# A fused low-rank update on one core: loads of four tiles, and the two small matrices on another queue

## The chip, the cores and the metric

The kernel runs on one core of one Trainium2 chip. The metric is the device time of one execution in microseconds (us). It is taken from plain runs; the profile comes from one further execution, which has a time of its own.

## The reference, cut to what matters

```python
def reference(x, A, B, scale):
    lora = np.matmul(np.matmul(x, A), B)
    return (x + scale * lora).astype(np.float32)
```

x is 16 x 512 x 768 in float32, that is 8192 rows of 768 numbers. A is 768 x 16, B is 16 x 768, scale is 0.5. All of x is read once and an output of the same size is written once, 25.2 MB each way.

## The kernel before, in words

**Tiles and parts.** The 8192 rows make 64 tiles of 128 rows. All 64 stay in one SBUF buffer, `xs`, from their load to their store; no space is used twice, except that three tiles of the last load hold A, a transposed A and B until these have been converted. The tiles are grouped in six parts (`PARTS`, L14: 2, 6, 8, 16, 16, 16 tiles). Inside a part, partition p holds consecutive rows of x (`rows`, L77), so a load of n tiles moves one contiguous run of n x 3 KB for each of the 128 partitions. `LOADS` (L15) says how many tiles each load brings: 2, 6 and then seven times 8. `STORES` (L16) says in which order the parts are written back: part 2, 1, 0, 3, 4, 5, one store for each.

**Chunks.** The arithmetic runs over 16 chunks of 4 tiles. For each chunk: three casts of `xs` to float16 (`xh`, one for each 256 columns, L108; GpSimd does nearly all of them); 24 transposing matmuls against an identity (`xt_ps`, L212); six copies of the result to SBUF by ScalarE (`xt`, L168); six matmuls with A (`yt_ps`, L223); one scaled copy by ScalarE (`yt`, L159); eight matmuls with B, two for each tile (`lo_ps`, L232); and four additions by VectorE, which add `lo_ps` into `xs` in place (L191). TensorE's order is written out by hand (L238 to L269), the middle of it a loop over chunks.

**The first chunk.** Its three casts go to three engines at once: GpSimd (columns 0 to 255), VectorE (256 to 511, L175), ScalarE (512 to 767, L155). `narrowed` (L97) makes an engine wait for every load that holds a tile of the chunk, the first time that this engine needs that load. Before, chunk 0 has its tiles in loads 0 and 1.

**A and B.** GpSimd first zeroes the place of A (`a_rows`, L112, the first count of the semaphore `zeroed`). Then A and B are loaded. VectorE transposes A (L178), casts it in four pieces (`a_mm`, L183) and casts B (`b_mm`, L188). The last of these raises `prep`. TensorE's first matmul with A waits for `prep`, and so does the last load, since it overwrites the three borrowed tiles.

**Queues.** All transfers are issued by SyncE, in this order: load 0, load 1, a wait for `zeroed`, A, B, loads 2 to 7, a wait for `prep`, load 8, and then the six stores, each after a wait until its part has been summed (`added`, raised by VectorE at L195). Transfers that one engine issued start on the 16 DMA engines in the order of issue. GpSimd's last act is to wait for all stores (L150).

ScalarE's program starts at L153 with a wait for the identity and a one-column copy that draws its table load to the front; its cast for chunk 0 comes next. VectorE's program starts with the cast for chunk 0 (L175) and goes on with A and B.

Of the kernel before, what the change touches and what calls it, by code (L numbers as in the profile page):

```python
# [10 lines left out]

PARTS = [2, 6, 8, 16, 16, 16]  # L14
LOADS = [2, 6, 8, 8, 8, 8, 8, 8, 8]  # L15
STORES = [2, 1, 0, 3, 4, 5]  # L16

CHUNK = 4
# [3 lines left out]
def kernel(  # L22
# [8 lines left out]
    nc = tc.nc  # L31
# [14 lines left out]
    NB = D // 32  # L46
    assert D % W == 0 and sum(LOADS) == NT == sum(PARTS) and sorted(STORES) == list(range(len(PARTS)))
    n_splits = [(n0, min(512, D - n0)) for n0 in range(0, D, 512)]
# [20 lines left out]

    room = NT - LOADS[-1]  # L70
    a_rows = xs[0:32, room, 0 : 32 * R].rearrange("b (a r) -> b a r", r=R)
    a_t = xs[0:32, room + 1, 0 : 32 * R].rearrange("a (r b) -> a r b", r=R)
    b_f32 = xs[0:R, room + 2, :]

    starts = [sum(PARTS[:i]) for i in range(len(PARTS))]

    def rows(t2, t0, n):  # L77
        i = max(i for i in range(len(PARTS)) if starts[i] <= t0)
        part = t2[ds(starts[i] * P, PARTS[i] * P), :].rearrange("(p s) d -> p s d", s=PARTS[i])
        return part[:, ds(t0 - starts[i], n), :]  # L80

    with tc.tile_critical():  # L82
# [3 lines left out]
        S = {k: nc.alloc_semaphore(name=f"s_{k}") for k in names}  # L86
        landed = [nc.alloc_semaphore(name=f"s_load{i}") for i in range(len(LOADS))]
        stored = nc.alloc_semaphore(name="s_stored")
        part_of = [i for i, n in enumerate(LOADS) for _ in range(n)]

        def load(i):
            t0, n = sum(LOADS[:i]), LOADS[i]
            nc.sync.dma_start(out=xs[:, t0 : t0 + n, :], in_=rows(x2, t0, n)).then_inc(landed[i], 16)  # L93
# [3 lines left out]
        def narrowed(engine, c, u):  # L97
            for i in sorted({part_of[c * CHUNK + s] for s in range(CHUNK)}):
                if (engine.engine, i) not in known:
                    known.add((engine.engine, i))  # L100
                    engine.wait_ge(landed[i], 16)  # L101
            src = xs[:, ds(c * CHUNK, CHUNK), ds(u * W, W)]
            if c >= 1:
                engine.wait_ge(S["turned"], ND * (c - 1) + 2 * u + 2)
            if engine is nc.scalar:
                i = engine.copy(out=xh[u], in_=src)  # L106
            else:
                i = engine.tensor_copy(out=xh[u], in_=src)  # L108
            i.then_inc(S[f"fed{u}"], 1)
# [6 lines left out]
            out=ident, in_=ident, compare_op=mybir.AluOpType.not_equal, fill=1.0,  # L116
# [4 lines left out]
        nc.gpsimd.memset(yt, 0.0).then_inc(S["zeroed"], 1)  # L121


        load(0)
        load(1)
        nc.sync.wait_ge(S["zeroed"], 1)
        nc.sync.dma_start(
            out=a_rows[0:NB, :, :], in_=A.rearrange("(b a) r -> b a r", a=32)
        ).then_inc(S["a"], 16)
        nc.sync.dma_start(out=b_f32, in_=B).then_inc(S["b"], 16)  # L130
        for i in range(2, len(LOADS) - 1):
            load(i)
        nc.sync.wait_ge(S["prep"], 1)
        load(len(LOADS) - 1)
# [1 line left out]
        for i in STORES:  # L136
            t0, n = starts[i], PARTS[i]
            if i + 1 > summed_parts:
# [3 lines left out]
                out=rows(out2, t0, n), in_=xs[:, t0 : t0 + n, :]  # L142
# [7 lines left out]
        nc.gpsimd.wait_ge(stored, 16 * len(STORES))  # L150


        nc.scalar.wait_ge(S["ident"], 1)  # L153
        nc.scalar.copy(out=first, in_=ident[:, 0:1])  # L154
        narrowed(nc.scalar, 0, 2)  # L155
# [15 lines left out]

        ends = {sum(PARTS[: i + 1]) for i in range(len(PARTS))}
        for k in (0, 1, 3):
            nc.vector.sem_inc(S[f"freed{k}"], 1)
        narrowed(nc.vector, 0, 1)  # L175

        nc.vector.wait_ge(S["a"], 16)
        nc.vector.transpose(out=a_t, in_=a_rows.rearrange("b a r -> b r a")).then_inc(S["a_t"], 1)  # L178
# [3 lines left out]
        for k in range(4):  # L182
            nc.vector.tensor_copy(  # L183
                out=a_mm[ds(32 * k, 32), 0 : ND * R].rearrange("p (c r) -> p c r", r=R),
                in_=a_tv[:, k, :, :],
            )
        nc.vector.wait_ge(S["b"], 16)
        nc.vector.tensor_copy(out=b_mm[0:R, :], in_=b_f32).then_inc(S["prep"], 1)  # L188
        for k in range(NT):
            nc.vector.wait_ge(S["lora"], k + 1)  # L190
            nc.vector.tensor_tensor(  # L191
                out=xs[:, k, :], in0=xs[:, k, :], in1=lo_ps[k % 2], op=add
            ).then_inc(S[f"freed{(k + 2) % CHUNK}"], 1)
            if k + 1 in ends:
                nc.vector.drain().then_inc(S["added"], 1)  # L195
# [109 lines left out]
```

## Time and profile before

| | before |
|---|---|
| time, median of 3 runs | 124.5 us (124.44 to 124.58) |
| time of the profiled execution | 124.9 us |
| its span, first to last instruction | 123.1 us |
| around the span | 1.8 us |
| TensorE busy | 69.8 us, from slice 5 to slice 28 of 40 |
| VectorE, ScalarE, GpSimd busy | 60.0, 60.3, 51.1 us |
| DMA packets, bytes | 2231, 50.46 MB |
| share of the span in which the SyncE queue's packets were in work, mean of the 16 DMA engines | 96.3% |

The page of the profile gives each engine's busy time, then the span cut into 40 slices of 3.08 us with a digit for the busy tenths of each, then the DMA queues, the chain of work that ended last, groups of instructions by line, and the issues of transfers with the time from issue to landing. The trace behind it can be asked for a stretch of time: which instructions ran, how busy the DMA engines were and what they moved. In such a stretch a packet counts where it begins, so a short stretch can show a DMA share of more than 1. An average over the whole span hides that the kernel has stages with different limits, so the stages are looked at one by one.

### The profile page before, as it was taken

The numbers are of one execution on the slowest core, as the hardware profiler recorded it, in microseconds if no ns is written. First come the engines' busy times: TensorE is split into PE (matmuls) and PEld (weight loads), VectorE is DVE, ScalarE is ACT, GpSimd is POOL, SyncE is SP. The second block draws the span as 40 slices with busy tenths as digits, with TensorE's granted clock in tenths as the row PEclk, the third lists the DMA queues.
The fourth block names the chain that finished last, engine by engine and source line by source line (L and its number), as shares of the span: only waits on it lengthen the run. The fifth ranks groups of instructions, "written<-read, shape, count | busy, mean of one in ns | idle before, by whom it ended". The sixth has DMA issues, their size and how long they took to land.

```text
span 123.1 us, 1586 instructions
## 1 busy us (share of the span) xinstructions
PE 69.8 (57%) x608; PEld 42.9 (35%) x608; DVE 60.0 (49%) x71; ACT 60.3 (49%) x115; POOL 51.1 (42%) x56
## 2 busy tenths in 40 slices
PE   0000699999999999999999999973000000000000
PEld 0000556656666565666656665630000000000000
DVE  0002706879779877977897798779000000000000
ACT  4002569878987987798789779850000000000000
POOL 6102677678667767676786677100000000000000
PEclk9999999999999999999999999999755555555555
DMA  3999999999999999999999999999989979989970
GB/s 92 439 419 383 463 407 415 463 399 455 423 407 479 402 423 455 399 423 450 399 463 407 413 434 509 411 431 479 447 351 495 447 335 495 463 367 447 495 303 0
DMA packets 2231, 50.46 MB, mean 410 GB/s; under 512 B 268, under 2 KB 268, under 8 KB 564
## 3 DMA queue, kind: packets, MB, share of 16 engines
q1 hardware_dynamic: 2228, 50.43, 96.3%
q14 instruction: 3, 0.02, 0.0%
HBM read 25.26 MB, written 25.17 MB: 410 GB/s over the span
## 4 chain that ended last, share of the span: by engine, by line
PE 54%; DMA 8%; DVE 4%; ACT 1%; issue 1%; DVEq 1%; SPq 0%
PE lo_ps L232 20%; PE yt_ps L223 17%; PE xt_ps L212 17%; DMA xs<-in_x_dram 8%; DVE xs L191 2%; ACT xt L168 1%; DVE xs L178 1%; DVE a_mm L183 1%; DVEq L195 1%; ACT yt L159 0%; DVE b_mm L188 0%; SPq L93 0%; DVE xh L108 0%; SPq L300 0%; DVEq L101 0%
## 5 line engine op out<-in xcount | busy, mean ns | idle before, releaser
L191 DVE TENSOR_TENSOR xs<-xs,lo_ps 128x768 f32<-128x768 f32 x64 | 56.9, 950 | 14.9 <-PE lo_ps L232 14.7
L108 POOL CAST xh<-xs 128x1024 f16<-128x1024 f32 x46 | 48.6, 1057 | 25.3 <-PE xt_ps L212 16.3
L168 ACT CAST xt<-xt_ps 128x512 f16<-128x512 f32 x96 | 49.8, 578 | 4.1 <-PE xt_ps L212 1.7
L212 PE MATMUL xt_ps<-ident,xh 128*128 128x128 f16 x384 | 32.8, 223 | 13.2 <-POOL xh L108 13.2
L212 PEld LDWEIGHTS xt_ps<-ident,xh 128*128 128x128 f16 x384 | 27.6, 100 | 21.3 <-issue 13.7
L223 PE MATMUL yt_ps<-xt,a_mm 128*128 128x512 f16 x96 | 32.0, 384 | 0.2
L232 PE MATMUL lo_ps<-b_mm,yt 128*128 128x512 f16 (+1 forms) x128 | 29.1, 330 | 2.0 <-DVE xs L191 1.1
L223 PEld LDWEIGHTS yt_ps<-xt,a_mm 128*128 128x128 f16 x96 | 9.4, 98 | 11.3 <-ACT xt L168 5.4
L159 ACT ACTIVATE yt<-yt_ps 16x512 f16<-16x512 f32 x16 | 9.4, 587 | 7.8 <-PE yt_ps L223 7.8
L232 PEld LDWEIGHTS lo_ps<-b_mm,yt 128*128 128x128 f16 x128 | 8.6, 97 | 9.4 <-ACT yt L159 2.7
L108 DVE CAST xh<-xs 128x1024 f16<-128x1024 f32 x1 | 0.7, 694 | 11.5 <-DMA xs<-in_x_dram 11.5
L106 ACT CAST xh<-xs 128x1024 f16<-128x1024 f32 x1 | 1.0, 1045 | 9.1 <-DMA xs<-in_x_dram 9.1
L154 ACT ACT_TABLE_LOAD x1 | 1.3, 1283 | 0.9 <-SPq L82 0.9
L178 DVE STREAM_TRANSPOSE xs<-xs 32x512 f32<-32x512 f32 x1 | 1.0, 1040 | 0.0
L183 DVE CAST a_mm<-xs 32x96 f16<-32x96 f32 x4 | 0.9, 232 | 0.1
L120 POOL MEMSET b_mm<- 128x768 f16 x1 | 0.7, 738 | 0.0
L112 POOL MEMSET xs<- 32x512 f32 x1 | 0.5, 514 | 0.5 <-SPq L82 0.5
L188 DVE CAST b_mm<-xs 16x768 f16<-16x768 f32 x1 | 0.5, 548 | 0.0
L121 POOL MEMSET yt<- 128x512 f16 x1 | 0.5, 524 | 0.0
L115 POOL TENSOR_SCALAR_AFFINE_SELECT ident<-ident 128x128 f16<-128x128 f16 x1 | 0.3, 292 | 0.2 <-POOL ident L113 0.2
L119 POOL MEMSET a_mm<- 128x208 f16 x1 | 0.3, 272 | 0.0
L154 ACT COPY first<-ident 128x1 f16<-128x1 f16 x1 | 0.2, 194 | 0.0
(5 smaller groups left out, 0.6 us busy)
## 6 DMA issues: line engine op xcount, KB each, us to landing
xs<-in_x_dram SPq DMA_DIRECT2D x7, 3072.0 KB, 36.3
out_dram<-xs SPq DMA_DIRECT2D x3, 6144.0 KB, 38.0
out_dram<-xs SPq DMA_DIRECT2D x1, 3072.0 KB, 35.6
xs<-in_x_dram SPq DMA_DIRECT2D x1, 2304.0 KB, 10.0
out_dram<-xs SPq DMA_DIRECT2D x1, 2304.0 KB, 40.6
xs<-in_x_dram SPq DMA_DIRECT2D x1, 768.0 KB, 4.5
out_dram<-xs SPq DMA_DIRECT2D x1, 768.0 KB, 42.1
xs<-in_A_dram SPq DMA_DIRECT2D x1, 48.0 KB
```

The lines of the kernel that those rows point to most:

```text
L106: i = engine.copy(out=xh[u], in_=src)
L108: i = engine.tensor_copy(out=xh[u], in_=src)
L154: nc.scalar.copy(out=first, in_=ident[:, 0:1])
L159: nc.scalar.activation(out=yt[0:R, :], in_=yt_ps[0:R, :], func=mybir.ActivationFunctionType.Copy, scale=sc).then_inc(S["y"], 1)
L168: nc.scalar.copy(out=xt[j], in_=xt_ps[j % NX]).then_inc(S[f"got{j}"], 1)
L178: nc.vector.transpose(out=a_t, in_=a_rows.rearrange("b a r -> b r a")).then_inc(S["a_t"], 1)
L183: nc.vector.tensor_copy(out=a_mm[ds(32 * k, 32), 0 : ND * R].rearrange("p (c r) -> p c r", r=R), in_=a_tv[:, k, :, :],)
L191: nc.vector.tensor_tensor(out=xs[:, k, :], in0=xs[:, k, :], in1=lo_ps[k % 2], op=add).then_inc(S[f"freed{(k + 2) % CHUNK}"], 1)
L195: nc.vector.drain().then_inc(S["added"], 1)
L212: i = nc.tensor.matmul(xt_ps[j % NX][:, ds(s * P, P)], xh[u][:, s, ds(h * P, P)], ident, start=True, stop=True,)
L223: i = nc.tensor.matmul(yt_ps, a_mm[:, ds(j * R, P)], xt[j], start=(j == 0), stop=(j == ND - 1))
L232: i = nc.tensor.matmul(lo_ps[s % 2][:, ds(n0, w)], yt[:, ds(s * P, P)], b_mm[:, ds(n0, w)], start=True, stop=True,)
```

## The change

Five edits, given here as the diff with its context cut. The issue of A and B moves from SyncE's program to the head of ScalarE's, B first, since only A has to wait for the zeroed place. The first 40 tiles are loaded four at a time by ten loads and the remaining 24 by three loads of eight, so there are 13 loads in place of 9. The first three parts have 4, 4 and 8 tiles in place of 2, 6 and 8, so load 0 holds exactly chunk 0. VectorE's cast for chunk 0 moves behind its work on A and B. The number of stores and their order stay; the two small ones are of 4 and 4 tiles in place of 6 and 2. The last load still has eight tiles and waits for `prep`.

```diff
-PARTS = [2, 6, 8, 16, 16, 16]
-LOADS = [2, 6, 8, 8, 8, 8, 8, 8, 8]
+PARTS = [4, 4, 8, 16, 16, 16]
+LOADS = 10 * [4] + 3 * [8]
 STORES = [2, 1, 0, 3, 4, 5]
...
-        load(0)
-        load(1)
-        nc.sync.wait_ge(S["zeroed"], 1)
-        nc.sync.dma_start(
-            out=a_rows[0:NB, :, :], in_=A.rearrange("(b a) r -> b a r", a=32)
-        ).then_inc(S["a"], 16)
-        nc.sync.dma_start(out=b_f32, in_=B).then_inc(S["b"], 16)
-        for i in range(2, len(LOADS) - 1):
+        for i in range(len(LOADS) - 1):
             load(i)
         nc.sync.wait_ge(S["prep"], 1)
         load(len(LOADS) - 1)
...
+        nc.scalar.dma_start(out=b_f32, in_=B).then_inc(S["b"], 16)
+        nc.scalar.wait_ge(S["zeroed"], 1)
+        nc.scalar.dma_start(
+            out=a_rows[0:NB, :, :], in_=A.rearrange("(b a) r -> b a r", a=32)
+        ).then_inc(S["a"], 16)
         nc.scalar.wait_ge(S["ident"], 1)
         nc.scalar.copy(out=first, in_=ident[:, 0:1])
         narrowed(nc.scalar, 0, 2)
...
-        narrowed(nc.vector, 0, 1)
...
         nc.vector.tensor_copy(out=b_mm[0:R, :], in_=b_f32).then_inc(S["prep"], 1)
+        narrowed(nc.vector, 0, 1)
         for k in range(NT):
```

## The prediction, made before the changed kernel ran

> **What bounds the kernel now.** I read the slices of the span first, then the issues of transfers, then single stretches. The page's slices:
>
> ```profile
> PE   0000699999999999999999999973000000000000
> ...
> DMA  3999999999999999999999999999989979989970
> GB/s 92 439 419 383 463 407 415 463 399 455 423 407 479 402 423 455 399 423 450 399 463 407 413 434 509 411 431 479 447 351 495 447 335 495 463 367 447 495 303 0
> ```
>
> TensorE starts in slice 5 and is done in slice 28. The DMA engines work from slice 2 to slice 39 with hardly a gap, so the transfers set the time and the arithmetic lies beside them. To see where the transfers lose time I add to each issue its time to landing. The page's list groups them:
>
> ```profile
> xs<-in_x_dram SPq DMA_DIRECT2D x7, 3072.0 KB, 36.3
> out_dram<-xs SPq DMA_DIRECT2D x3, 6144.0 KB, 38.0
> out_dram<-xs SPq DMA_DIRECT2D x1, 3072.0 KB, 35.6
> xs<-in_x_dram SPq DMA_DIRECT2D x1, 2304.0 KB, 10.0
> out_dram<-xs SPq DMA_DIRECT2D x1, 2304.0 KB, 40.6
> xs<-in_x_dram SPq DMA_DIRECT2D x1, 768.0 KB, 4.5
> out_dram<-xs SPq DMA_DIRECT2D x1, 768.0 KB, 42.1
> ```
>
> Asked in narrow stretches, the trace gives each one alone. Issue plus time to landing, in us: load 0 0.94+4.5 = 5.4; load 1 1.38+10.0 = 11.4; B 2.34+9.4 = 11.7; loads 2 to 7 at 18.8, 26.1, 33.4, 40.7, 48.3, 55.6; load 8 14.73+49.2 = 63.9; stores of parts 2, 1, 0 at 71.2, 76.6, 78.6; of parts 3, 4, 5 at 93.1, 107.5 and 86.52+35.5 = 122.0. I call this the ladder. A large store is a step of 14.5 us for 16 tiles, so two tiles (768 KB) cost 1.81 us, and all 128 tile transfers 116.0 us. The other 6.0 us before 122.0 are: 0.94 before the first issue; 3.2 at the start (11.4 - 0.94 - 4 x 1.81); 0.3 for A and B; 1.05 in load 8's step (8.3 for 7.25); 0.35 in load 6's (7.6); 0.2 in part 0's store (2.0 for 1.81); rounding. Then come 1.1 us to the span's end and 1.8 around it: 124.9 us for the profiled execution. The median of the plain runs is 0.4 lower, 124.5, and I carry that difference over.
>
> Two places in the ladder matter. The first is the start, seen in stretches (columns: length, five engines, clock, DMA share, GB/s):
>
> ```profile
> 0.00:2.00 2.00, 0.00 (x0) 0.00 (x0) 0.00 (x0) 1.09 (x1) 1.03 (x7) 1.00 0.06 9
> 2.00:4.00 2.00, 0.00 (x0) 0.00 (x0) 0.00 (x0) 0.38 (x2) 1.48 (x4) 1.00 0.92 313
> 10.00:12.00 2.00, 0.00 (x0) 0.00 (x0) 0.51 (x1) 0.53 (x1) 0.48 (x1) 1.00 1.20 424
> 91.50:106.00 14.50, 0.00 (x0) 0.00 (x0) 0.00 (x0) 0.00 (x0) 0.00 (x0) 0.50 1.00 434
> ```
>
> The last row is the norm: share 1.00 for 434 GB/s. From 10 to 12 us, where load 2's first packets follow the small ones of A and B, share 1.20 bought 424; 424/434 would be 0.98, so packets took 0.22 x 2 = 0.44 us longer than they should. The second place is load 8. Asked for 55.6 to 64 us, the queues answer:
>
> ```profile
> q1 hardware_dynamic: 159, 3.51, 99.6%
> q14 instruction: 1, 0.01, 0.2%
> ```
>
> One of the three instruction packets on the page came in this stretch; the second came in load 6's stretch, the third at 72 to 77 us. Both late loads have one. A landing waits for the slowest of 16 engines, so one delayed engine shows in full, and later steps do not win it back.
>
> **The change, part by part.**
>
> *A and B off the middle.* Their step, 0.3 us, goes. They must still ride somewhere: until 2 us the engines are dark (share 0.06), and from 2 to 4 us a share of 0.08, 0.16 us, is idle. All in the dark would save 0.3, interleaved with load 0 nothing. B is issued at about 0.9 us, beside load 0; A waits for `zeroed` (GpSimd's first memset on `xs` ends at 1.46) and B's issue (0.34), so its 0.43 us issue ends near 1.9 and its packets come after load 0's first. I take -0.2. The Trainium skill, "DMA: Bandwidth & Descriptors", section "Issuing engines are not separate DMA queues", speaks against this edit: transfers from several engines interleave on the same 16, and a second issuer saves only issue time. By that rule this term is 0 and the sum 0.2 higher; no run here has two issuers yet.
>
> *The slow packets behind them.* With no small packets ahead of a large load in mid-queue, the 0.44 us should go; or they follow A and B into the start (0), or come on top of its slow packets (+0.4). I take -0.4, since packets from 2 to 4 us are slow already (share 0.92 for 313 GB/s).
>
> *Four more transfers, in smaller packets.* Loads 9 to 13; stores stay 6 (two of 1536 KB for 2304 and 768; 5.4+2.0 against 7.25, so 0 to -0.1). Price of one more: a 768 KB step exceeded its size by 0.2, a 3072 KB step by 0.05. 1536 KB lies between, and the eight packets of each DMA engine are what both share; nearer the larger row, 0.075. Four make +0.3; ends +0.2 and +0.8.
>
> *First transfers of four tiles for 2 and 6.* Of the start's 3.2 us, load 0 holds 2.7 (4.5 - 1.81) and load 1 0.5. I take 0; the 0.5 could go or double.
>
> *The chunk-0 chain.* Load 0 lands near 5.4 + 1.81 = 7.2 us; before, all three casts waited until 11.4. VectorE now does A and B first: 1.04 + 0.97 + 0.55 = 2.6 us, then its 0.69 us cast. If A and B land by 4.5 that is hidden; if they land with load 0, the cast ends at 10.5. TensorE starts at 9 to 10.5 instead of 13.2, so all sums come 2.5 to 4 us earlier, worth 0: part 5's store is issued at 86.5 while its forerunner lands at 107.5 (cover 21 us), part 2's at 35.6 while load 8 lands at 63.9 (28 us).
>
> *Queues.* SyncE: twelve loads at a median 0.45 us are issued by about 6.4 us, then it waits for `prep` as now (the waits of its queue give `SPq L93 <- DVE b_mm L188` 8.9 us); the last load has over 40 us of queued loads ahead of it, so cost 0. ScalarE: its wait for `zeroed` and two issues push the table load (1.28 us, now at 0.91) to about 1.9, ending near 3.2; behind it are the identity copy, the cast for load 0 (7.2) and every evacuation: 4 us of cover, cost 0. VectorE: behind its wait for A stand the cast and all additions, behind the cast TensorE; priced above.
>
> *The last-load delay.* Its 1.05 us I leave as it is (0). Instruction packets will come at other times, for the arithmetic runs ahead, and may meet other DMA engines: -1.0 to +1.0.
>
> **Sum:** -0.2 - 0.4 + 0.3 = -0.3. Profiled execution 124.9 - 0.3 = 124.6, median **124.2 us**.
>
> **Rivals.**
>
> 1. *The late engine is spared* (0.17). If no instruction packet strikes an engine that is late already, load 8's step falls to 7.3: another -0.7 to -1.0, about 123.4. For it: steps without such a packet are 7.3. Against: three packets came in the span and the program isn't shorter.
>
> 2. *Two queues at the start, slower* (0.25). Place: the DMA engines at 2 to 6 us, where small packets of the ScalarE queue alternate with load 0's. Price: the 0.4 us of slow packets stays, the 0.3 step isn't saved, the transfers cost +0.3 to +0.8: 124.8 to 125.3. It decides once B's packets get to the engines no sooner than load 0's, so that none rides in the dark. For it: both issues start at 0.91 to 0.94.
>
> 3. *A later delay* (0.08): an instruction packet strikes the last engine once more, +1.0 on the forecast: 125.2. Against: only two of the ladder's steps show it.
>
> 4. *A fixed time for every transfer* (0.02). By the widest row, 0.2 each, it would be the +0.8 above. The Trainium skill, same page, "Anatomy of one DMA", fits 2.0 us plus bytes at 436 GB/s per transfer on the GpSimd path; four would be an estimated 8 us, if nothing overlaps. The trace speaks against that: 3072 KB steps are 7.3 us, and the fit would make them about 9.2.
>
> 5. *Nothing moves* (0.10): what is saved ahead is lost again to the slowest engine, 124.3 to 124.7.
>
> **How the numbers follow.** The forecast has the remaining 0.38, own range 123.9 to 124.6. A measurement of this kernel can tell about 0.2%, 0.25 us, from no change. Below 124.25 lie rival 1 (0.17) and 0.25 of the forecast: faster 0.42. Within: 0.13 of the forecast, 0.10 of rival 5, 0.04 of rival 2's lower end: same 0.27. Slower: 0.21 of rival 2, rivals 3 and 4: 0.31. The range from 123.3 (rival 1) to 125.2 (rivals 2 and 3) leaves out about 2 in 10: larger moves of the delays, the wide ends of the start, and rival 4.
>
> **What the changed profile would show.** In the ladder: load 0 near 7.2 us, the first eight tiles (loads 0 and 1) near 11.4, 16 tiles near 18.3 instead of 18.8; steps of 1536 KB at 3.7; large stores still 14.5 apart. In the stretches: no surplus of DMA share around 10 to 12 us. TensorE's first matmul at 9 to 10.5. Wrong if the 16 tiles land later than 18.8 (rival 2), if steps of 1536 KB are over 3.8 (packets), or if the last load's step isn't 8.3 (instruction packets). What would overturn all of it is a gap in the DMA row before the last store, for then transfers no longer set the time.

## The result, and the profile after

The changed kernel is slower: 124.97 us in the median of 8 runs (124.47 to 125.11), against 124.47 us for 8 runs of the kernel before beside it. The ratio is 1.0032 with a 95% interval of 1.0019 to 1.0046. A second set of 5 runs, taken later with other kernels, gave 124.84 us and 1.0037 (1.0024 to 1.0051). The forecast was 124.2, a gain of 0.3; it became a loss of 0.4 to 0.5.

The slices of the changed kernel's page, as before: the arithmetic starts a slice earlier, and the DMA engines still work from slice 2 to slice 39.

```profile
PE   0007999999999999999999999750000000000000
...
DMA  3999999999999999999999999999999899899890
GB/s 74 400 403 437 413 429 433 421 429 421 425 429 419 457 457 409 441 427 417 441 427 425 401 429 481 469 449 433 401 481 449 369 481 449 385 449 465 385 449 0
```

The list of transfers on the same page (KB each, median us to landing):

```profile
out_dram<-xs SPq DMA_DIRECT2D x3, 6144.0 KB, 40.3
xs<-in_x_dram SPq DMA_DIRECT2D x10, 1536.0 KB, 21.0
xs<-in_x_dram SPq DMA_DIRECT2D x3, 3072.0 KB, 45.6
...
xs<-in_B_dram ACTq DMA_DIRECT2D x1, 48.0 KB, 4.0
```

B lands 4.0 us after its issue instead of 9.4. The profiled execution was one of the eight runs and the lowest of them, 124.47 us with a span of 122.7. The kernel before had been profiled in an execution of 124.9 us, above all its plain runs. Two single profiles would therefore have told the wrong story, so both kernels were profiled again. The ladder (issue plus time to landing, us) of the two further profiles of the kernel before and of both of the changed kernel:

| landed | before, 2nd and 3rd profile | changed, 1st and 2nd |
|---|---|---|
| 8 tiles | 11.37, 11.54 | 11.53, 11.61 |
| 16 tiles | 18.81, 18.96 | 18.91, 18.98 |
| 40 tiles | 40.72, 40.87 | 41.35, 41.36 |
| 64 tiles | 63.25, 63.39 | 63.66, 63.82 |
| last store | 121.47, 121.54 | 121.64, 121.96 |
| time of the execution | 124.29, 124.36 | 124.47, 124.78 |

At 16 tiles, where a gain of 0.5 had been forecast, the kernels are level. Between 16 and 40 tiles, where the changed kernel loads fours and the other eights, it falls behind by 0.5. After that the gap shrinks, to 0.42 at 64 tiles and 0.30 at the last store (means of two), and these four executions differ by 0.30 in time. They lie below the medians of their sets, those of the changed kernel further on average.

### The profile page after: what moved, and what is told of

It reads as the page before. It is cut to its first block, busy times and chain, and to the rows that moved or that the text cites. A ratio compares the mean times of both kernels' runs of the same rounds, so it can differ in the third digit from the quotient of the medians.

```text
span 122.7 us, 1592 instructions
## 1 busy us (share of the span) xinstructions
PE 70.7 (58%) x608; PEld 43.4 (35%) x608; DVE 59.9 (49%) x71; ACT 60.5 (49%) x115; POOL 50.4 (41%) x56
## 4 chain that ended last, share of the span: by engine, by line
PE 56%; DMA 5%; DVE 5%; DVEq 1%; issue 1%; ACT 0%; POOL 0%; POOLq 0%; SPq 0%
PE lo_ps L230 20%; PE xt_ps L210 18%; PE yt_ps L221 18%; DMA xs<-in_A_dram 5%; DVE xs L189 2%; DVE xs L175 1%; DVE a_mm L180 1%; DVEq L193 1%; DVE xh L108 1%; ACT yt L157 0%; DVE b_mm L185 0%; POOL xs L112 0%; POOLq L298 0%; POOL ident L113 0%; SPq L82 0%
## 5 line engine op out<-in xcount | busy, mean ns | idle before, releaser
L108 POOL CAST xh<-xs 128x1024 f16<-128x1024 f32 x46 | 47.9, 1042 | 23.4 <-PE xt_ps L210 19.0
L210 PE MATMUL xt_ps<-ident,xh 128*128 128x128 f16 x384 | 33.5, 225 | 10.0 <-POOL xh L108 9.1
L221 PE MATMUL yt_ps<-xt,a_mm 128*128 128x512 f16 x96 | 32.6, 395 | 0.0
```

The source lines that it names most:

```text
L210: i = nc.tensor.matmul(xt_ps[j % NX][:, ds(s * P, P)], xh[u][:, s, ds(h * P, P)], ident, start=True, stop=True,)
L221: i = nc.tensor.matmul(yt_ps, a_mm[:, ds(j * R, P)], xt[j], start=(j == 0), stop=(j == ND - 1))
```

## The experiments

Times are medians; "before" is the kernel before, run beside each (124.39 to 124.48 us).

### Is it the queue or the loads?

Three kernels part the change. The first only moves A and B:

```diff
@@ the kernel before
-        nc.sync.wait_ge(S["zeroed"], 1)
-        nc.sync.dma_start(out=a_rows[0:NB, :, :], ...)
-        nc.sync.dma_start(out=b_f32, in_=B).then_inc(S["b"], 16)
...
+        nc.scalar.dma_start(out=b_f32, in_=B).then_inc(S["b"], 16)
+        nc.scalar.wait_ge(S["zeroed"], 1)
+        nc.scalar.dma_start(out=a_rows[0:NB, :, :], ...)
         nc.scalar.wait_ge(S["ident"], 1)
```

> The kernel before with one edit: A and B are issued at the head of ScalarE's program instead of between SyncE's loads 1 and 2. Theory (the small transfers bring their slow packets with them wherever they go, and smaller loads cost the rest): 16 tiles land at 18.6 to 19.0 us as before (18.81), the median stays within 0.2 us of before. Rival (two issuing queues at the start are what makes the changed kernel slower): 16 tiles land at 19.2 or later and the median is 0.3 to 0.5 us above before.

Measured: 124.89 us, 1.0038 (1.0025 to 1.0051). 16 tiles land at 18.90. Each theory got half: the landing is the one's, the time the rival's. It was profiled a second time; see Repeats.

The second only changes the loads and the parts:

```diff
@@ the kernel before
-PARTS = [2, 6, 8, 16, 16, 16]
-LOADS = [2, 6, 8, 8, 8, 8, 8, 8, 8]
+PARTS = [4, 4, 8, 16, 16, 16]
+LOADS = 10 * [4] + 3 * [8]
```

> The kernel before with the new PARTS and LOADS alone; A and B stay on SyncE's queue behind the first two loads (again eight tiles). Theory (smaller loads cost): each 1536 KB load steps by 3.69 us instead of 3.65, in sum +0.3 for the loads, and the median is 0.25 to 0.5 us above before, the whole of the change's loss. Rival (two queues): within 0.15 us of before.

Measured: 124.90 us, 1.0041 (1.0028 to 1.0054); 16 tiles at 19.12, steps of 3.69, 40 tiles at 41.26. The loads alone cost what the whole change costs, as the theory said. The two halves do not add up, though: each costs 0.4 to 0.5 us, and so do both together.

The third keeps everything of the change but the many small loads:

```diff
@@ the changed kernel
-LOADS = 10 * [4] + 3 * [8]
+LOADS = [4, 4, 8, 8, 8, 8, 8, 8, 8]
```

> The changed kernel with loads of 4, 4 and then seven times 8 tiles, so that only the first two loads are small; A and B on ScalarE's queue, parts as in the changed kernel. Theory (smaller loads cost): steps of 3072 KB at 7.3 us, 16 tiles near 18.8, the median within 0.2 us of before. Rival (two queues): the median stays 0.3 to 0.5 us above before.

Measured: 124.53 us, 1.0014 (1.0005 to 1.0022), steps of 7.30, 16 tiles at 18.89. With these loads, two issuing queues are not what costs. Its twin has the same loads and A and B on SyncE's queue:

```diff
@@ the kernel before
-PARTS = [2, 6, 8, 16, 16, 16]
-LOADS = [2, 6, 8, 8, 8, 8, 8, 8, 8]
+PARTS = [4, 4, 8, 16, 16, 16]
+LOADS = [4, 4, 8, 8, 8, 8, 8, 8, 8]
```

> The kernel before with parts of 4, 4, 8, 16, 16, 16 and loads of 4, 4 and seven times 8 tiles; A and B stay on SyncE's queue behind the first two loads. Beside the kernel with the same loads and A and B on ScalarE's queue (0.14% above before) it prices the move of A and B alone. Theory (the move of A and B gains nothing): 124.4 to 124.7, within 0.2 us of that one. Rival (the move gains the predicted 0.6): 124.9 to 125.2.

Measured: 124.58 us, 1.0008 (0.9999 to 1.0017), 16 tiles at 19.07. Beside the third kernel this prices the move of A and B with loads of four in front: the 16 tiles land 0.18 us earlier with the move, and the time does not tell the two apart. The Trainium skill ("DMA: Bandwidth & Descriptors", "Issuing engines are not separate DMA queues") says that a second issuer saves issue time only. These two runs agree with it; the first kernel of this section, 0.4 to 0.5 us slower by the same move, does not follow from it (Repeats has what cost it).

### What small loads cost

```diff
@@ the changed kernel
-LOADS = 10 * [4] + 3 * [8]
+LOADS = 28 * [2] + [8]
```

> The changed kernel with 28 loads of two tiles and one of eight in place of ten of four and three of eight. Theory (a fixed cost for each transfer and packet): a 768 KB step of 1.865 to 1.885 us, in sum about 1 us more than the changed kernel, median 125.7 to 126.1. Rival (the loss of the changed kernel is in its late steps and not in the number of loads): median within 0.3 us of the changed kernel, 124.7 to 125.2.

Measured: 125.77 us, 1.0102 (1.0087 to 1.0118), in the page's list

```profile
xs<-in_x_dram SPq DMA_DIRECT2D x28, 768.0 KB, 21.1
```

and in the ladder steps of 1.88 almost throughout. So the same eight tiles cost 7.30 us as one load, 2 x 3.69 = 7.38 as two and 4 x 1.88 = 7.52 as four: 0.07 to 0.08 us for each further transfer, which is eight more packets for each of the 16 engines. Sixteen more transfers than in the changed kernel took 0.93 us, 0.06 each. The fit of the Trainium skill (same page, "Anatomy of one DMA", 2.0 us and the bytes for each transfer, stated for the GpSimd path) would have made that an estimated 32 us; for transfers that stand in a queue the trace does not bear it out.

Does the price also run the other way?

```diff
@@ the changed kernel
-LOADS = 10 * [4] + 3 * [8]
+LOADS = [4, 4, 8, 16, 16, 8, 8]
```

> The changed kernel with fewer, larger loads: 4, 4, 8, 16, 16, 8, 8 tiles. Theory (cost by transfer and packet): 6144 KB steps of 14.5 us, 16 tiles near 18.9, median 124.2 to 124.5, level with before or a little below. Rival (two issuing queues cost whatever the loads are): 124.8 or more.

Measured: 124.97 us, 1.0040 (1.0026 to 1.0054): missed. The first load of 16 tiles took the expected 14.54, the second, with an instruction packet in it, 14.97, and all 64 tiles had landed at 62.83, earlier than in either kernel. But the stores' steps were 7.45, 3.87, 3.90 and 15.16, together 1.2 us over the changed kernel's second profile (7.29, 3.63, 3.63, 14.60). Chunk 4 now waits for a load of 16 tiles, the arithmetic ends later (the last store is issued at 93.2 instead of 83.8), and I read from this that late steps which go with the arithmetic fall into the stores; no run here separates it. So late steps had to be understood.

### What makes single steps late

Each of the profiles so far has three packets of the instruction queue in its span, and the steps with the first two of them are late. The next kernel lengthens SyncE's program where SyncE is idle. The 1024 waits leave 512 more instructions in the trace, 545 on SyncE for 33:

```diff
@@ the changed kernel
         load(len(LOADS) - 1)
+        for _ in range(1024):
+            nc.sync.wait_ge(S["prep"], 1)
```

> The changed kernel with 512 more instructions on SyncE between the last load and the stores, waits that are long satisfied. They move no data and SyncE is idle there; they only make its instruction stream longer, so that four more instruction packets of 8 KB come by the DMA engines. Theory (an instruction packet makes the engine that carries it late, and the slowest engine sets the end): instruction packets 3 to about 7, new late steps of 0.2 to 0.7 us between 14 and 45 us, and the median up by 0.5 to 2 us, the more of them fall on one engine. Rival (instruction packets are harmless and the late steps have another cause): the median stays within 0.2 us of the changed kernel.

Measured: 127.27 us, 1.0235 (1.0220 to 1.0249), 2.4 us over the changed kernel. Its page's queues:

```profile
q1 hardware_dynamic: 2736, 50.33, 94.3%
q10 hardware_dynamic: 68, 0.10, 0.6%
q14 instruction: 7, 0.06, 0.1%
```

There are 7 instruction packets for 3 and no other byte more. 0.6 us for each is far more than the 0.3 us that 8 KB takes: in the trace the engine's next data packet, too, takes about 0.4 us longer. All four struck the same engine, as the ends show: one engine finished 2.46 us after the last but one, and the others no later than in the changed kernel's second profile (121.28 us against 121.45), where the two last engines finish within 0.05. The theory's mechanism held; the 2.4 us are above its range of 0.5 to 2.

Then I tried to take the third packet away, by moving nine casts from GpSimd, whose program fetches it, to VectorE:

```diff
@@ the kernel before, GpSimd's loop and VectorE's
-                if c >= 1 or u == 0:
+                if (c >= 1 or u == 0) and c < NC - 3:
                     narrowed(nc.gpsimd, c, u)
...
                 nc.vector.drain().then_inc(S["added"], 1)
+            if (k + 1) % CHUNK == 0 and NC - 3 <= (k + 1) // CHUNK + 1 < NC:
+                for u in range(NU):
+                    narrowed(nc.vector, (k + 1) // CHUNK + 1, u)
```

> The kernel before with the casts of the last three chunks moved from GpSimd to VectorE, ahead of the additions of the chunk before each; GpSimd's program is ten instructions shorter. Theory (an instruction packet delays the engine that carries it, and the third one, at 62 to 74 us, is fetched for GpSimd's program, since it came earlier wherever GpSimd had more waits): two instruction packets in the span instead of three, and the median 0.1 to 0.5 us below before. Rival (the third belongs to another program, or its engine is not the last to finish): three packets, or two and no change within 0.1 us.

Measured: 124.85 us, 1.0037 (1.0025 to 1.0048). The page counts two instruction packets in the span; the third, which had come at 73.9 us, now comes at 123.3, after the span's end, so it was GpSimd's. The last store lands as before (121.57), so its engine had not been the last. But the span ends 1.43 us after that landing instead of 1.04: in the closing steps GpSimd clears the semaphores 0.38 us after its drain instead of 0.03. That it waits there for instructions is my reading and not shown; the packet at 123.3 comes only after the clearing. Neither the forecast gain nor the rival's tie came.

How much does the arithmetic cost the transfers in all? Here the second half of it is left out; tiles 32 to 63 are stored as they were loaded:

```diff
@@ the kernel before
-    NC = NT // CHUNK
+    NC = NT // CHUNK // 2
...
-        for k in range(NT):
+        for k in range(NC * CHUNK):
             nc.vector.wait_ge(S["lora"], k + 1)
...
+                if t0 + n <= NC * CHUNK:
                     nc.sync.wait_ge(S["added"], summed_parts)
+                else:
+                    for q in sorted(set(part_of[t0 : t0 + n])):
+                        nc.sync.wait_ge(landed[q], 16)
```

> The kernel before with the arithmetic of the first eight chunks alone; the other 32 tiles are loaded and stored as they are, so the output lacks their low-rank term. All transfers stay, and the arithmetic lies beside them in any case. Theory (the arithmetic costs time only through the DMA engines: instruction packets, and one engine whose packets are 5% longer from about 60 us until the arithmetic ends): at most one instruction packet in the span, no stretch of long packets after 60 us, the last store lands 0.6 to 1.2 us earlier than in the kernel before, median 123.3 to 123.9. Rival (the late engines have nothing to do with the arithmetic): 124.3 to 124.5.

Measured: 124.28 us, 0.9985 (0.9975 to 0.9995). One instruction packet is left, and the last store lands at 121.01, 0.5 earlier than in the two later profiles of the kernel before. But only 0.2 of it shows in the time, since the time around the span was 2.2 us instead of 1.8. The theory missed its size in both, the landing (0.6 to 1.2) and the time, which is all but the rival's 124.3. What was absent is the single late engine after 62 us; longer packets on many engines at 59 to 62 us came here too.

### The price of A and B in both places

```diff
@@ the changed kernel, ScalarE
-        nc.scalar.dma_start(out=b_f32, in_=B).then_inc(S["b"], 16)
         nc.scalar.wait_ge(S["zeroed"], 1)
-        nc.scalar.dma_start(out=a_rows[0:NB, :, :], ...)
+        nc.scalar.sem_inc(S["a"], 16)
@@ GpSimd, ahead of the zeroing of A's place
+        nc.gpsimd.memset(b_f32, 0.0).then_inc(S["b"], 16)
```

> The changed kernel without the transfers of A and B: their places are zeroed by GpSimd and the waits are raised without data, so the low-rank term is 0 and the output is x. Theory (A and B cost about 0.3 us for their bytes and as much for slow packets beside them, also on ScalarE's queue): 16 tiles land at 18.2 to 18.4 us instead of 18.91 and the median falls by 0.5 to 0.7 us against the changed kernel, to 0.1 to 0.3 below before. Rival (they ride where the engines are dark and cost nothing): 16 tiles at 18.9, median as the changed kernel, 0.3 to 0.5 above before.

Measured: 124.24 us, 0.9990 (0.9980 to 0.9999), 0.6 below the changed kernel's 124.84. 8 tiles land at 10.77 instead of 11.53 and 11.61, and 16 tiles at 18.46: the next two steps took 3.90 and 3.79 for 3.69, with longer packets on many engines at 13 to 16 us. So A and B still cost 0.8 us at eight tiles when they go by ScalarE's queue, of which this profile loses 0.3 again to something else. The same omission in the kernel before:

```diff
@@ the kernel before, SyncE
         nc.sync.wait_ge(S["zeroed"], 1)
-        nc.sync.dma_start(out=a_rows[0:NB, :, :], ...)
-        nc.sync.dma_start(out=b_f32, in_=B).then_inc(S["b"], 16)
+        nc.sync.sem_inc(S["a"], 16)
@@ GpSimd, ahead of the zeroing of A's place
+        nc.gpsimd.memset(b_f32, 0.0).then_inc(S["b"], 16)
```

> The kernel before without the transfers of A and B (their places are zeroed, so the low-rank term is 0 and the output is x). It prices A and B in the middle of SyncE's queue, as the same omission in the changed kernel priced them on ScalarE's queue: there 16 tiles landed 0.45 to 0.5 us earlier and the median fell by 0.6. Theory (they cost the same in both places, so that moving them could gain nothing): 16 tiles at 18.3 to 18.4 us instead of 18.8 to 19.0, the surplus of DMA share at 10 to 12 us gone, median 123.8 to 124.0. Rival (in the middle they cost more, as forecast): 16 tiles at 18.1 or earlier, median 123.7 or less. Other rival (in the middle they cost less): 16 tiles at 18.6 or later.

Measured: 124.42 us, 0.9995 (0.9985 to 1.0006), 16 tiles at 18.18, 0.63 earlier. The landing is between the theory's and the rival's, and the time is neither's: next to nothing of the 0.63 was left at the end. By the landings, A and B cost about as much here (0.6 to 0.8, over all profiles) as on ScalarE's queue. A second profile of it:

> The kernel before without the transfers of A and B once more, unedited, for a second profile (output x). In the first, 16 tiles landed 0.63 us earlier and the last load's step took 8.83 us instead of 7.8, so that nothing was left of the gain at the end. Theory (the gain is regularly lost again before the stores): the last load's step is 8.4 to 9 us again and the time 124.3 to 124.5 us. Rival (a chance of that profile): the step is 7.5 to 7.9 us and the time 123.7 to 123.9.

Measured: 124.37 us; 16 tiles at 18.12, and the last load's step 8.77 after 8.83 in the first. It is regular. The stretch from 58 to 62 us, first in the second profile of the kernel before, then in the two profiles without A and B (DMA share and GB/s at the end):

```profile
58.00:62.00 4.00, 3.99 (x38) 2.40 (x36) 3.31 (x5) 3.36 (x8) 3.06 (x3) 1.00 1.01 424
```

```profile
58.00:62.00 4.00, 3.99 (x37) 2.42 (x36) 3.31 (x4) 3.36 (x8) 2.89 (x4) 1.00 1.08 350
```

```profile
58.00:62.00 4.00, 3.99 (x39) 2.52 (x37) 3.31 (x5) 3.36 (x7) 2.92 (x3) 1.00 1.04 338
```

At no lower a share of busy time, 350 and 338 GB/s instead of 424 for 4 us are 0.7 to 0.8 us of transfer lost, about what had been ahead. Packets of many engines are longer there, not those of one: 31 took over 930 ns in each of the two. The kernel before has some too (14, 12 and 7 in its three profiles), the changed kernel 1 and 0. The changed kernel without A and B does not show the loss, and keeps its gain:

```profile
58.00:62.00 4.00, 3.99 (x39) 2.52 (x38) 3.47 (x4) 3.37 (x8) 2.95 (x4) 1.00 1.00 426
```

So, as far as these profiles show, the slow stretch goes with the kernel before and is worse there without A and B. What causes it, I could not find; it stays open.

### Repeats

> The changed kernel once more, unedited, for a second profile and for times beside the next three. Theory (the slowest DMA engine's late steps vary from run to run, and the first profile caught a lucky one): median 124.8 to 125.0; 16 tiles land at 18.8 to 19.0 and 1536 KB steps are 3.69 again; the late steps beyond that sum to 0.9 to 1.3 us instead of 0.7 if the profiled run is a usual one. Rival (the start or the steps vary): the surplus over the first profile sits in the first 16 tiles or in the plain steps.

Measured: 124.84 us; 16 tiles at 18.98, steps of 3.69; late steps 3.92 for 3.69, 7.89 for 7.30 and 14.60 for 14.49, 0.93 in sum. The first profile had 0.29 + 0.45 = 0.74. The theory held, barely.

> The kernel before, unedited, for a second profile. The first one was of an execution of 124.9 us, above all plain runs. Theory (the packets of many DMA engines that were slow at 60 to 62 us in that profile were a single disturbance): 124.3 to 124.7 us, load 8's step 7.7 to 7.9 instead of 8.3, the first 16 tiles again at 18.8, the rest as in the first profile. Rival (load 8's late step belongs to this kernel): 8.2 or more again.

> The kernel before once more, unedited, for a third profile; the same expectations as for the second: 124.3 to 124.7 us, load 8's step 7.7 to 7.9, 16 tiles at 18.8.

Measured: 124.29 and 124.36 us, load 8's step 7.80 and 7.85, 16 tiles at 18.81 and 18.96. The 8.3 of the first profile held half a microsecond that did not come again. The longer packets themselves did, on many engines in all three profiles; that half of the theory is refuted.

> The kernel before with A and B at the head of ScalarE's program, unedited from its first run, for a second profile. It was 0.38% above before although 16 tiles landed as before. Theory (the engine that carries the first instruction packet is already among the latest in this kernel): the step with the packet near 40 us is 7.8 to 8.1 us again, where the kernel before has 7.4 to 7.6, and the median 124.75 to 124.95. Rival (chance of that run): that step 7.4 to 7.6 and the median near 124.5.

Measured: 124.85 us, 1.0029 (1.0018 to 1.0039), and the step with the instruction packet near 40 us is 8.02 after 8.03 in the first profile. In the kernel before the first such packet adds 0.07 to 0.25 to its step (7.37 to 7.56), in this one 0.7. That packet costs its engine 0.69 us (309 ns, and 0.38 on the data packet behind it). If the last engine to land is the one that carried it, it would without the packet have landed at 40.86 and 40.68 us here, level with the next (40.83 and 40.69), but in the kernel before at 47.45 and 47.54, level with the first of all (47.36 and 47.47). By this, moving A and B alone costs what it does because the engine that carries the packet is then already among the latest; why the move makes it so, no run shows.

## Why the prediction was wrong, point by point

**What bounds the kernel** was read rightly: transfers throughout, and 2.6 us earlier stores (part 5's at 83.9 for 86.5) gained nothing.

**"A and B off the middle", -0.2, and "the slow packets behind them", -0.4: these steps failed.** They were to gain 0.6 us and to land 16 tiles near 18.3; the changed kernel landed them at 18.91 and 18.98, 0.06 later than the kernel before (means of two profiles each) and later than the 18.8 that the prediction had named as its sign of being wrong. Taken alone, moving A and B gained 0.03 where loads of 2 and 6 tiles stand in front (18.86 to 18.83, means of three and two profiles) and 0.2 where fours do (19.12 to 18.91 and 18.98, and 19.07 to 18.89). The other 0.2 is what A and B behind two loads of four cost more than behind 2 and 6, although eight tiles land no later there (11.28 and 11.38); "First transfers of four tiles" had taken 0. Profiles of one kernel differ by 0.15, so these shares are rough. The surplus at 10 to 12 us did go, in the changed kernel:

```profile
10.00:12.00 2.00, 1.11 (x8) 0.75 (x8) 0.92 (x2) 1.15 (x3) 0.42 (x1) 1.00 1.00 424
```

But over the whole start nothing was saved. The stretch from 2 to 12 us, in the second profile of the kernel before:

```profile
2.00:12.00 10.00, 0.00 (x0) 0.00 (x0) 0.53 (x1) 0.93 (x3) 1.98 (x5) 1.00 1.02 402
```

In the changed kernel:

```profile
2.00:12.00 10.00, 2.04 (x15) 1.52 (x16) 3.17 (x7) 3.98 (x6) 2.94 (x6) 1.00 1.00 387
```

In the kernel before without A and B, then in the changed kernel without them:

```profile
2.00:12.00 10.00, 0.00 (x0) 0.00 (x0) 1.04 (x2) 1.43 (x3) 2.94 (x7) 1.00 1.03 425
```

```profile
2.00:12.00 10.00, 3.12 (x23) 2.45 (x24) 3.19 (x7) 4.67 (x7) 4.67 (x9) 1.00 0.98 398
```

By the prediction's norm (434 GB/s for share 1.00) the surplus is (1.02 - 402/434) x 10 = 0.9 us in the first, 1.1 in the second, 0.5 in the third and 0.6 in the fourth. The slow packets hang on A and B and moved with them. Nor did these ride in the dark. B was issued at 0.91, load 0 at 0.94; load 0's packets start at 1.96 and B's only at 2.9 (q10 is ScalarE's queue). The changed kernel's queues, asked for 2.8 to 4 us:

```profile
q1 hardware_dynamic: 30, 0.37, 83.7%
q10 hardware_dynamic: 29, 0.05, 11.7%
```

A, issued at 1.49, has its packets between 5.4 and 6.6 us:

```profile
q1 hardware_dynamic: 34, 0.41, 90.4%
q10 hardware_dynamic: 26, 0.05, 10.9%
```

That was rival 2's condition word for word, "once B's packets get to the engines no sooner than load 0's", and its 124.8 to 125.3 holds the result. But the condition does not decide it: in the kernel with the lengthened SyncE program B was issued 0.05 us ahead of load 0, its first packets came at 1.96 and load 0's at 2.11, and 16 tiles still landed at 18.82. And what makes rival 2's number is the +0.3 for small loads that the forecast had too; with larger loads two queues cost little (124.53). I gave rival 2 0.25 and the forecast 0.38, although the one row that bore on its condition, both issues within 0.03 us of each other, spoke for it. The Trainium skill, "DMA: Bandwidth & Descriptors", "Queues, rings and completion order", says that an engine drains a whole packet, typically 9 to 17 descriptors, from one ring before it turns to another. The trace does not bear that count out here: load 0 has eight packets on each engine, 128 in all, and B's packets begin when 14 to 38 packets of the loads have begun, one or two on each engine, A's when 94 to 122 have. A small transfer on a second queue is in any case not first by being small.

**"Four more transfers, in smaller packets", +0.3**, was right. The 24 tiles between 16 and 40 cost 6 x 3.69 instead of 3 x 7.30, +0.24, and the run with loads of two tiles gave 0.06 to 0.08 for each transfer where 0.075 was taken. With four more loads the median rose from 124.58 to 124.90 with A and B on SyncE's queue, and from 124.53 to 124.84 and 124.97 on ScalarE's.

**"The last-load delay", 0**: in sum right, its reading half wrong. Three instruction packets in both kernels, at nearly the same cost: the late steps sum to 0.80 and 0.74 us in the kernel before (2nd and 3rd profile) and to 0.74 and 0.93 in the changed one, whose last load's step is 7.24 and no longer late; the load ahead of it is (7.75, 7.89). In the changed kernel the first falls into the loads of four (steps of 3.98 and 3.92), 0.26 late, where the kernel before loses 0.07 to 0.25. Half of the 1.05 us that I had read off load 8 did not come again in two further profiles.

**The chunk-0 chain and the queues**: costs 0, as said. TensorE starts at 9.07. SyncE, however, did not issue twelve loads by 6.4 us: the tenth issue took 1.7 us, and each later one, begun at 7.6, 10.8 and 14.1 us, 3.2 us instead of 0.4 to 0.5. With 40 us of loads ahead it cost nothing.

**The sum** with what was measured in the ladder: +0.06 at the start, +0.24 for small loads, +0.07 for late steps: +0.37, where the last store lands 0.30 later. The medians differ by 0.43 to 0.50. The rest is not placed, since the profiled executions of the changed kernel were 0.06 to 0.5 us below their medians; what their late steps are in the usual execution, no profile shows. And a gain at the start is not always kept: without A and B the kernel before is 0.63 us ahead at 16 tiles and level at the end, while the changed kernel keeps its 0.6.

## What to carry to other kernels

In this kernel, which keeps the DMA engines busy throughout, two small transfers cost slow neighbours as well as their bytes, 0.6 to 0.8 us in all, and they took both along to where they were moved. Before counting on an idle place, look in the trace when packets would get there and not when they are issued. Splitting queued loads costs little each (0.07 us here) but buys nothing when the arithmetic has 20 us of cover. For changes below half a per cent, take several profiles of each kernel: a single execution here was off by as much as the effect.

## What the runs showed of the hardware that I had not expected

- An instruction packet of 8 KB delayed the DMA engine that carried it by about 0.6 us, and a longer program on an idle engine therefore slowed transfers: 512 more instructions on SyncE, 4 packets, +2.4 us.
- The data packet behind the first, second and third instruction packet was longer by 0.38, 0.66 and 0.2 us in both kernels, to within 0.05.
- From about 62 us until the arithmetic ends, packets that follow one another, by their times on one engine, are some 5% longer than the rest (945 to 996 ns for 24,576 bytes, elsewhere mostly 912 to 920). With half the arithmetic this was absent.
- In the changed kernel SyncE issued nine loads of four tiles in 0.4 to 0.9 us each; the tenth's issue took 1.7 to 1.9 us and each of the three after it 3.2.
